# Weight sums of a seven-product feed-forward made by accumulating transfers, and a fourth pair of chunks by seven products

## The chip, the cores and the metric

The kernel runs on one core of a Trainium2 chip. The metric is the device time of one execution in microseconds, and the time of a kernel is the median of several executions. One execution was also taken by the hardware profiler; all rows below come from that one.

## The reference, cut to what matters

The program is a two-layer decoder trunk for 256 tokens of width 1024. Each layer has a feed-forward step, a token mixer, and a second feed-forward step, so there are four feed-forward stages with weights of their own. They are what the change touches.

```python
def swiglu(h, w_gate, w_up, w_down):
    return (jax.nn.silu(h @ w_gate) * (h @ w_up)) @ w_down

def rmsnorm(x, g):
    y = xf * lax.rsqrt(jnp.mean(xf * xf, axis=-1, keepdims=True) + RMS_EPS)
    return (y * g.astype(jnp.float32)).astype(x.dtype)

    f = swiglu(rmsnorm(x, g[0]), ffn_w_gate[layer, 0], ffn_w_up[layer, 0], ffn_w_down[layer, 0])
    x = x + 0.5 * rmsnorm(f, g[1])
    ... # token mixer
    f = swiglu(rmsnorm(x, g[4]), ffn_w_gate[layer, 1], ffn_w_up[layer, 1], ffn_w_down[layer, 1])
    x = x + 0.5 * rmsnorm(f, g[5])
```

The inner width is 2816, everything is float32.

## The kernel before, in words

**Units.** The inner width is cut into 11 chunks of 256. A chunk's gate and up columns together are 512 wide. The 256 tokens are two tiles of 128, called t = 0 and 1. The contraction over 1024 is eight slices of 128.

**Precision.** A float32 operand is split into `hi` (rounded by ScalarE, line 96) and `lo` (the rest, by VectorE, line 97). A product is three matmuls for each slice: hi·hi, hi·lo, lo·hi (`mm3`, lines 145 to 147, and `product`, lines 334 to 336). So each weight block of 512 x 512 that is loaded, 1 MiB, costs two ScalarE and two VectorE instructions of 128 x 1024 before TensorE can use it.

**Buffers.** A loaded block lies in one of five `raw` buffers of 1 MiB (`NRAW`), filled by two transfers of 512 KB (gate, up) on SyncE's queue (line 87). The `hi` and `lo` halves have nine slots each (`NW`); a block takes two of each. Products gather in two PSUM banks with the tag `mm`.

**Chunks done plainly.** `GU(t, c)` makes chunk c for token tile t: 8 slices x 3 = 24 matmuls of 128 x 512. `both` does it for both tiles, 48 matmuls, from two loaded blocks. Then `gated` makes silu(gate)·up, `T` transposes it on TensorE, and `Dn(t, c)` multiplies it by the chunk's rows of `w_down` (12 matmuls; the rows are one more block of 1 MiB for each chunk) into PSUM banks that gather over the whole stage.

**Pairs of chunks done by seven products.** For two neighbouring chunks a and b the token tiles are the rows, the halves of the contraction the middle, and the chunks the columns of a 2 x 2 block product. `M(i, a)` for i = 0 to 6 makes it by seven block products of 12 matmuls, 84 in place of 96. They need sums of weight blocks. With b11, b21 the two halves of chunk a and b12, b22 those of chunk b, VectorE makes four sums of 128 x 2048 for each pair, in place in the raw buffers:

```python
                nc.vector.tensor_tensor(w["b12"], w["b22"], w["b12"], op=ALU.subtract)   # L358, i == 1
                nc.vector.tensor_tensor(w["b11"], w["b12"], w["b11"], op=ALU.add)        # L359, i == 1
                nc.vector.tensor_tensor(w["b12"], w["b22"], w["b11"], op=ALU.subtract)   # L374, i == 4
                nc.vector.tensor_tensor(w["b21"], w["b21"], w["b11"], op=ALU.subtract)   # L382, i == 5
```

The sums of the token blocks (`S`) are made once for each stage. Results that are shared between outputs are combined on VectorE from PSUM (128 x 512: lines 364, 372, 379, 386, 392).

**Order.** `PAIRS = ((2, 3), (5, 6), (8, 9))`: chunks 0, 1, 4, 7, 10 are plain, so that a plain chunk stands between two pairs. A planner in `ffn` (`emit`, `settle`) writes out the order of `M`, `GU`, `T` and `Dn` from prices of each step (M 1, GU 2, both 4, Dn 1), so that a `Dn` comes between products. The framework's scheduler then gives each engine its queue, close to that order, and puts in the semaphore waits. GpSimd (POOL) has in the feed-forward stages only the power of each norm (line 182), and issues no transfer; all weights go over SyncE's queue.

Of the kernel before, what the change touches and what calls it, by code (L numbers as in the profile page):

```python
# [17 lines left out]
P = 128  # L18
# [16 lines left out]

PAIRS = ((2, 3), (5, 6), (8, 9))
SIDE, EARLY = 13, 5
# [11 lines left out]
def trunk(ctx, tc, x, norm_g, w_gate, w_up, w_down, ab_in, ab_out, conv_w, conv_b, conv_g, conv_bb,  # L49
# [10 lines left out]
    def ps_mm(name):  # L60
        return pp.tile([P, 512], F32, tag="mm", name=name, bufs=2)
# [58 lines left out]

    def load_block(l, j, c, half):

        def loads(raw):
            v = raw.rearrange("p (k g f) -> p k g f", k=4, g=2)
            return [(v[:, :, g, :], w[l, j, half * 512:half * 512 + 512, c * FC:(c + 1) * FC].rearrange("(k p) f -> p k f", p=P))
                    for g, w in ((0, w_gate), (1, w_up))]
        return load(loads, f"b{l}{j}_{c}_{half}")

# [121 lines left out]
    def ffn(l, j, pre, tail, hooks=()):  # L250
# [60 lines left out]


        S = {}

        def sums():
            (a11, a12), (a21, a22) = pre[0][3], pre[1][3]
            for n, dst, x, y, op in ((1, a22, a21, a22, ALU.add), (3, a21, a11, a21, ALU.subtract),
                                     (2, a11, a22, a11, ALU.subtract), (4, a12, a12, a11, ALU.subtract)):
                nc.vector.tensor_tensor(dst, x, y, op=op)
                d = sp.tile([P, 8, P], F32R, tag=f"S{n}" if n < 4 else "tg", name=f"S{n}_{l}{j}", bufs=1)  # L320
                split(dst, d[:, 0:4].rearrange("p a b -> p (a b)"), d[:, 4:8].rearrange("p a b -> p (a b)"))
                S[n] = (d[:, 0:4], d[:, 4:8])

# [14 lines left out]
        def M(i, a):  # L338
            b = a + 1
            n = f"{l}{j}_{a}"  # L340
            if i == 0:
                if not S:
                    sums()
                w = W[a] = {}
                w["m"] = sp.tile([P, 2, 512], F32, tag="cacc", name=f"m{n}")
                w["u"] = sp.tile([P, 2, 512], F32, tag="hpad", name=f"u{n}")
                w["b11"] = load_block(l, j, a, 0)
                units = split_raw(w["b11"], f"b11_{n}")
                w["b22"] = load_block(l, j, b, 1)
                w["b12"] = load_block(l, j, b, 0)  # L350
                w["X"] = ps_mm(f"gX{n}")
                product(w["X"], block(0, 0), units, True, False)
                nc.scalar.activation(w["m"][:, 0], w["X"], AF.Copy)
                return
            w = W[a]
            m1, m5, u1, u2 = w["m"][:, 0], w["m"][:, 1], w["u"][:, 0], w["u"][:, 1]
            if i == 1:
                nc.vector.tensor_tensor(w["b12"], w["b22"], w["b12"], op=ALU.subtract)  # L358
                nc.vector.tensor_tensor(w["b11"], w["b12"], w["b11"], op=ALU.add)  # L359
                units = split_raw(w["b11"], f"t2_{n}")  # L360
                w["b21"] = load_block(l, j, a, 1)
                w["Y"] = ps_mm(f"gY{n}")
                product(w["Y"], S[2], units, True, False)
                nc.vector.tensor_tensor(u1, w["Y"], m1, op=ALU.add)
            elif i == 2:
                units = split_raw(w["b21"], f"b21_{n}")
                product(w["X"], block(0, 1), units, False, True)
                gated(0, a, w["X"])
            elif i == 3:
                units = split_raw(w["b12"], f"t3_{n}")  # L370
                product(w["Y"], S[3], units, False, False)
                nc.vector.tensor_tensor(u2, w["Y"], m1, op=ALU.add)
            elif i == 4:
                nc.vector.tensor_tensor(w["b12"], w["b22"], w["b11"], op=ALU.subtract)  # L374
                units = split_raw(w["b12"], f"t1_{n}")
                w["X2"] = ps_mm(f"gX2{n}")
                product(w["X2"], S[1], units, True, False)
                nc.scalar.activation(m5, w["X2"], AF.Copy)
                nc.vector.tensor_tensor(u2, u2, m5, op=ALU.add)
                gated(1, b, u2)  # L380
            elif i == 5:
                nc.vector.tensor_tensor(w["b21"], w["b21"], w["b11"], op=ALU.subtract)  # L382
                units = split_raw(w["b21"], f"t4_{n}")
                product(w["Y"], block(1, 1), units, False, True)
                c = sp.tile([P, 512], F32, tag="va", name=f"c21_{n}", bufs=2)
                nc.vector.tensor_tensor(c, w["Y"], m1, op=ALU.add)
                gated(1, a, c)
            else:
                units = split_raw(w["b22"], f"b22_{n}")
                product(w["X2"], S[4], units, False, True)  # L390
                c = sp.tile([P, 512], F32, tag="va", name=f"c12_{n}", bufs=2)
                nc.vector.tensor_tensor(c, w["X2"], u1, op=ALU.add)
                gated(0, b, c)

# [9 lines left out]
        G.append((GU, 0, e))  # L404
        makes = {2: (0, 0), 4: (1, 1), 5: (1, 0), 6: (0, 1)}
        price = {M: 1.0, GU: 2.0, both: 4.0, T: 0.1, Dn: 1.0}
# [510 lines left out]
```

## Time and profile before

| | |
|---|---|
| median of 3 runs | 992.99 us |
| lowest and highest run | 986.86 and 993.05 us |
| the profiled execution's own time | 989.26 us |
| its span, first to last instruction | 987.3 us |
| mean granted TensorE clock | 0.994 |
| busy: TensorE, VectorE, ScalarE, GpSimd | 953.1, 837.7, 579.4, 97.7 us |
| moved over SyncE's queue | 174.5 MB |

The profiled execution's time lies 2.0 us above its span, and 3.7 us below the median. Busy times of TensorE count matmuls that overlap as pipelined, so an issue distance is read from starts that follow one another, not from durations.

### The profile page before, as it was taken

What the parts mean: (1) busy time and instruction counts of PE and PEld (TensorE: products, weight loads), DVE (VectorE), ACT (ScalarE), POOL (GpSimd) and SP (SyncE); (2) the same over time, 40 slices, a digit from 0 to 9 for tenths busy, and PEclk for the clock granted to TensorE, in tenths of its full rate; (3) what the DMA queues carried; (4) which work ended last, traced back from release to release, by engine and by line L of the source; (5) the groups of instructions that cost most, each with busy time, mean ns of one, the idle gap of its engine ahead of it and who ended that gap; (6) DMA issues with size and microseconds to landing.
All of it is one profiled execution on the core that took longest, in us unless ns stands there. A gap on an engine that the chain in (4) does not pass through costs nothing.

```text
span 987.3 us, 11853 instructions
## 1 busy us (share of the span) xinstructions
PE 953.1 (97%) x4350; PEld 759.0 (77%) x4352; DVE 837.7 (85%) x1022; ACT 579.4 (59%) x845; POOL 97.7 (10%) x104
## 2 busy tenths in 40 slices
PE   7999999999888999999999999999999989999997
PEld 5777888787657688878778887877787778887875
DVE  6999999679887999988789999996757489999883
ACT  7575656563535656656576756575555466656561
POOL 0100000039961000000000000000000010000000
PEclk9999999999989999999999999999999999999999
DMA  9657647456007339383862658385564142838341
GB/s 313 209 184 230 218 167 282 161 177 232 1 18 239 91 107 315 122 262 121 284 213 86 200 183 275 109 311 162 209 220 144 43 127 86 275 120 288 107 168 43
DMA packets 121754, 175.32 MB, mean 178 GB/s; under 512 B 4481, under 2 KB 96321, under 8 KB 121696
## 3 DMA queue, kind: packets, MB, share of 16 engines
q1 hardware_dynamic: 121536, 174.50, 53.7%
q8 instruction: 34, 0.56, 0.2%
q14 instruction: 24, 0.20, 0.1%
q10 hardware_dynamic: 160, 0.07, 0.0%
HBM read 173.50 MB, written 1.05 MB: 177 GB/s over the span
## 4 chain that ended last, share of the span: by engine, by line
PE 84%; DVE 8%; ACT 3%; DMA 2%; issue 2%; POOL 1%; SPq 0%; POOLq 0%; DVEq 0%; ACTq 0%
PE f L145 8%; PE f L146 8%; PE f L147 8%; PE gu L147 6%; PE gu L145 6%; PE gu L146 6%; PE gX L334 4%; PE gX L336 4%; PE gX L335 4%; PE gY L334 3%; PE gY L335 3%; PE gY L336 3%; PE hT L153 2%; PE cd L145 2%; PE cd L146 2%
## 5 line engine op out<-in xcount | busy, mean ns | idle before, releaser
L145 PE MATMUL f<-hi_dn,hs 128*128 128x512 f32 x352 | 139.7, 400 | 0.5 <-ACT hs L157 0.5
L146 PE MATMUL f<-lo_dn,hs 128*128 128x512 f32 x352 | 138.0, 392 | 0.0
L147 PE MATMUL f<-hi_dn,hs 128*128 128x512 f32 x352 | 137.5, 393 | 0.0
L96 ACT ACTIVATE hi_t<-raw_b 128x1024 fp32r<-128x1024 f32 x96 | 98.1, 1053 | 60.2 <-DVE raw_b L374 47.1
L97 DVE TENSOR_TENSOR lo_t<-raw_b,hi_t 128x1024 fp32r<-128x1024 f32 x96 | 114.5, 1220 | 14.5 <-ACT hi_t L96 14.5
L97 DVE TENSOR_TENSOR lo_dn<-raw_dn,hi_dn 128x1024 fp32r<-128x1024 f32 x88 | 105.7, 1219 | 9.0 <-ACT hi_dn L96 8.9
L96 ACT ACTIVATE hi_dn<-raw_dn 128x1024 fp32r<-128x1024 f32 x88 | 91.7, 1055 | 36.4 <-PE gu L147 26.2
L97 DVE TENSOR_TENSOR lo_gu<-raw_gu,hi_gu 128x1024 fp32r<-128x1024 f32 x80 | 96.6, 1218 | 8.3 <-ACT hi_gu L96 8.0
L96 ACT ACTIVATE hi_gu<-raw_gu 128x1024 fp32r<-128x1024 f32 x80 | 83.5, 1055 | 27.9 <-PE m L147 11.7
L97 DVE TENSOR_TENSOR lo_b<-raw_b,hi_b 128x1024 fp32r<-128x1024 f32 x72 | 86.3, 1219 | 2.5 <-ACT hi_b L96 2.3
L96 ACT ACTIVATE hi_b<-raw_b 128x1024 fp32r<-128x1024 f32 x72 | 74.8, 1057 | 21.4 <-PE gu L147 12.9
L145 PEld LDWEIGHTS f<-hi_dn,hs 128*128 128x128 f32 x352 | 65.7, 188 | 17.2 <-ACT hs L157 4.4
L147 PEld LDWEIGHTS f<-hi_dn,hs 128*128 128x128 f32 x352 | 66.1, 188 | 15.3 <-DVE hs L158 1.7
L146 PEld LDWEIGHTS f<-lo_dn,hs 128*128 128x128 f32 x352 | 66.2, 188 | 13.8 <-DVE lo_dn L97 1.0
L157 ACT ACTIVATE hs<-hT 128x256 fp32r<-128x256 f32 x88 | 32.2, 377 | 54.9 <-PE hT L153 54.9
L145 PE MATMUL gu<-hi_gu,xh_l1f 128*128 128x512 f32 x160 | 63.6, 397 | 0.0
L146 PE MATMUL gu<-lo_gu,xh_l1f 128*128 128x512 f32 x160 | 63.4, 396 | 0.0
L147 PE MATMUL gu<-hi_gu,xl_l1f 128*128 128x512 f32 x160 | 62.2, 393 | 0.0
L158 DVE TENSOR_TENSOR hs<-hT,hs 128x256 fp32r<-128x256 f32 x88 | 36.0, 418 | 20.4 <-ACT hs L157 20.0
L282 ACT ACTIVATE sg<-gu 128x256 f32<-128x256 f32 x38 | 14.5, 381 | 42.1 <-PE gu L147 39.3
L334 PE MATMUL gY<-hi_t,S 128*128 128x512 f32 x96 | 38.6, 402 | 0.0
L336 PE MATMUL gY<-hi_t,S 128*128 128x512 f32 x96 | 38.0, 396 | 0.0
(361 smaller groups left out, 2240.7 us busy)
## 6 DMA issues: line engine op xcount, KB each, us to landing
raw_dn<-in_ffn_w_down_dram SPq DMA_DIRECT2D x44, 1024.0 KB, 5.0
raw_b<-in_ffn_w_gate_dram SPq DMA_DIRECT2D x48, 512.0 KB, 4.7
raw_b<-in_ffn_w_up_dram SPq DMA_DIRECT2D x48, 512.0 KB, 6.2
raw_gu<-in_ffn_w_gate_dram SPq DMA_DIRECT2D x38, 512.0 KB, 4.2
raw_gu<-in_ffn_w_up_dram SPq DMA_DIRECT2D x38, 512.0 KB, 5.2
raw_ab<-in_ab_w_in_dram SPq DMA_DIRECT2D x10, 1024.0 KB, 6.9
raw_cd<-in_cd_w_in_dram SPq DMA_DIRECT2D x10, 1024.0 KB, 5.1
raw_abo<-in_ab_w_out_dram SPq DMA_DIRECT2D x4, 1024.0 KB, 5.5
```

The lines of the kernel that those rows point to most:

```text
L96: nc.scalar.activation(hi, r, AF.Copy)
L97: nc.vector.tensor_tensor(lo, r, f32v(hi), op=ALU.subtract)
L145: nc.tensor.matmul(ps, xh, wh, start=first, stop=False)
L146: nc.tensor.matmul(ps, xh, wl, start=False, stop=False)
L147: nc.tensor.matmul(ps, xl, wh, start=False, stop=last)
L153: nc.tensor.transpose(ps[:, i * P:(i + 1) * P], src[:, i * P:(i + 1) * P], ident)
L157: nc.scalar.activation(hi, ps, AF.Copy)
L158: nc.vector.tensor_tensor(lo, ps, f32v(hi), op=ALU.subtract)
L282: nc.scalar.activation(sg, ps[:, 0:FC], AF.Silu, scale=1.0 if r is None else r)
L334: nc.tensor.matmul(ps, A[0][:, k, :], wh[:, o], start=first and k == 0, stop=False, **tc_skip)
L335: nc.tensor.matmul(ps, A[0][:, k, :], wl[:, o], start=False, stop=False, **tc_skip)
L336: nc.tensor.matmul(ps, A[1][:, k, :], wh[:, o], start=False, stop=k == 3, **tc_skip)
```

## The change

Four things change at once.

1. `PAIRS` becomes `((2, 3), (4, 5), (6, 7), (8, 9))`: chunks 4 and 7, plain before, become part of pairs, and no plain chunk stands between pairs any more. This holds in all four feed-forward stages.
2. The sums change their signs (so that each weight sum is an addition), and three of the four sums of a pair are made by transfers with `accum_op=add`, issued from GpSimd's queue: `t = b12 + b11` (b12 loaded by SyncE, b11 added from HBM by two transfers of 512 KB), `b22 += b12` (again two from HBM), and `b21 += t` (one transfer of 1 MiB within SBUF). One sum, `t += b22`, stays on VectorE. So b11 and b12 are each read from HBM a second time: 2 MiB more for each pair.
3. The seven products come in another order: b11, t1, b21, b22, t2, t3, t4. The three that gather in one bank (`Y`) now follow one another, i = 4, 5, 6; before they were i = 1, 3, 5.
4. In SyncE's queue the load of b12 into `t` stands ahead of that of b11, and the three others follow at once in step 0.

```diff
-PAIRS = ((2, 3), (5, 6), (8, 9))
+PAIRS = ((2, 3), (4, 5), (6, 7), (8, 9))
...
+    def add_block(raw, l, j, c, half):
+
+        for dst, src in block_of(l, j, c, half)(raw):
+            tc.keep_in_program_order(nc.gpsimd.dma_start(dst, src, accum_op=ALU.add))
...
-            for n, dst, x, y, op in ((1, a22, a21, a22, ALU.add), (3, a21, a11, a21, ALU.subtract),
-                                     (2, a11, a22, a11, ALU.subtract), (4, a12, a12, a11, ALU.subtract)):
+            for n, dst, x, y, op in ((1, a22, a21, a22, ALU.subtract), (3, a21, a11, a21, ALU.subtract),
+                                     (2, a11, a22, a11, ALU.subtract), (4, a12, a12, a11, ALU.add)):
...
+                w["t"] = load_block(l, j, b, 0)
+                add_block(w["t"], l, j, a, 0)
                 w["b11"] = load_block(l, j, a, 0)
                 units = split_raw(w["b11"], f"b11_{n}")
+                w["b21"] = load_block(l, j, a, 1)
                 w["b22"] = load_block(l, j, b, 1)
-                w["b12"] = load_block(l, j, b, 0)
...
             if i == 1:
-                nc.vector.tensor_tensor(w["b12"], w["b22"], w["b12"], op=ALU.subtract)
-                nc.vector.tensor_tensor(w["b11"], w["b12"], w["b11"], op=ALU.add)
-                units = split_raw(w["b11"], f"t2_{n}")
-                w["b21"] = load_block(l, j, a, 1)
-                w["Y"] = ps_mm(f"gY{n}")
-                product(w["Y"], S[2], units, True, False)
-                nc.vector.tensor_tensor(u1, w["Y"], m1, op=ALU.add)
+                units = split_raw(w["t"], f"t1_{n}")
+                w["X2"] = ps_mm(f"gX2{n}")
+                product(w["X2"], S[1], units, True, False)
+                nc.scalar.activation(m5, w["X2"], AF.Copy)
...
             elif i == 3:
-                units = split_raw(w["b12"], f"t3_{n}")
+                units = split_raw(w["b22"], f"b22_{n}")
+                nc.vector.tensor_tensor(w["t"], w["t"], w["b22"], op=ALU.add)
+                add_block(w["b22"], l, j, b, 0)
+                tc.keep_in_program_order(nc.gpsimd.dma_start(w["b21"], w["t"], accum_op=ALU.add))
+                product(w["X2"], S[4], units, False, True)
+            elif i == 4:
+                units = split_raw(w["t"], f"t2_{n}")
+                w["Y"] = ps_mm(f"gY{n}")
+                product(w["Y"], S[2], units, True, False)
+                nc.vector.tensor_tensor(u1, w["Y"], m1, op=ALU.add)
+                gated(0, b, made(w["X2"], u1, ALU.subtract, "c12"))
+            elif i == 5:
+                units = split_raw(w["b22"], f"t3_{n}")
                 product(w["Y"], S[3], units, False, False)
                 nc.vector.tensor_tensor(u2, w["Y"], m1, op=ALU.add)
-            elif i == 4:
-                nc.vector.tensor_tensor(w["b12"], w["b22"], w["b11"], op=ALU.subtract)
-                units = split_raw(w["b12"], f"t1_{n}")
...
-                nc.vector.tensor_tensor(u2, u2, m5, op=ALU.add)
+                nc.vector.tensor_tensor(u2, m5, u2, op=ALU.subtract)
                 gated(1, b, u2)
-            elif i == 5:
-                nc.vector.tensor_tensor(w["b21"], w["b21"], w["b11"], op=ALU.subtract)
+            else:
                 units = split_raw(w["b21"], f"t4_{n}")
                 product(w["Y"], block(1, 1), units, False, True)
...
-        makes = {2: (0, 0), 4: (1, 1), 5: (1, 0), 6: (0, 1)}
+        makes = {2: (0, 0), 4: (0, 1), 5: (1, 1), 6: (1, 0)}
```

## Rows read from the trace of the kernel before

**Rows 1.** The page's head: span, and busy time of each engine.

```profile
span 987.3 us, 11853 instructions
...
PE 953.1 (97%) x4350; PEld 759.0 (77%) x4352; DVE 837.7 (85%) x1022; ACT 579.4 (59%) x845; POOL 97.7 (10%) x104
```

**Rows 2.** Windows of the four feed-forward stages: engines' busy time, clock, DMA share, GB/s.

```profile
24.70:214.00 189.30, 186.33 (x845) 149.38 (x845) 170.65 (x199) 113.84 (x163) 5.79 (x7) 1.00 0.61 206
320.00:505.00 185.00, 182.11 (x820) 145.64 (x819) 164.43 (x185) 115.53 (x168) 2.74 (x5) 1.00 0.57 184
505.00:690.00 185.00, 183.85 (x827) 147.81 (x825) 165.92 (x188) 114.94 (x164) 3.04 (x4) 1.00 0.60 194
790.00:987.30 197.30, 187.82 (x837) 151.15 (x835) 164.54 (x190) 112.89 (x163) 4.72 (x5) 0.99 0.46 152
```

**Rows 3.** Timeline of TensorE, first stage: one product's first matmul and the next step's.

```profile
151.90 0.40 PE L334 MATMUL gX<-hi_b,xh_l0n 128*128 128x512 f32 x1
...
154.65 0.39 PE L145 MATMUL f<-hi_dn,hs 128*128 128x512 f32 x1
```

**Rows 4.** Windows, third stage and second: pair with plain chunk; dense loads; no loads.

```profile
587.12:635.51 48.39, 48.29 (x217) 39.22 (x216) 44.26 (x46) 29.46 (x39) 0.00 (x0) 1.00 0.62 203
330.00:345.00 15.00, 15.00 (x71) 11.78 (x70) 14.09 (x20) 8.10 (x15) 0.55 (x1) 1.00 0.06 11
...
599.00:614.00 15.00, 15.00 (x68) 12.08 (x67) 14.55 (x18) 11.44 (x14) 0.00 (x0) 1.00 1.04 334
```

**Rows 5.** Groups of instructions, whole span: busy, mean ns, idle before.

```profile
L97 DVE TENSOR_TENSOR lo_t<-raw_b,hi_t 128x1024 fp32r<-128x1024 f32 x96 | 114.5, 1220 | 14.5 <-ACT hi_t L96 14.5
L96 ACT ACTIVATE hi_t<-raw_b 128x1024 fp32r<-128x1024 f32 x96 | 98.1, 1053 | 60.2 <-DVE raw_b L374 47.1 <-PE f L147 6.1 <-DVE raw_b L359 5.9
...
L158 DVE TENSOR_TENSOR hs<-hT,hs 128x256 fp32r<-128x256 f32 x88 | 36.0, 418 | 20.4 <-ACT hs L157 20.0
...
L359 DVE TENSOR_TENSOR raw_b<-raw_b,raw_b 128x2048 f32<-128x2048 f32 x12 | 27.5, 2289 | 0.2
...
L285 DVE TENSOR_TENSOR h<-c,sg 128x256 f32<-128x256 f32 x24 | 10.0, 418 | 0.0
...
L364 DVE TENSOR_TENSOR u<-gY,m 128x512 f32<-128x512 f32 x12 | 8.3, 688 | 0.0
```

**Rows 6.** The page's DMA issues: count, KB each, median us to landing.

```profile
raw_b<-in_ffn_w_gate_dram SPq DMA_DIRECT2D x48, 512.0 KB, 4.7
raw_b<-in_ffn_w_up_dram SPq DMA_DIRECT2D x48, 512.0 KB, 6.2
```

**Rows 7.** Timeline of SyncE's queue, third stage: first and last load of a pair.

```profile
604.45 0.37 SPq L87 DMA_DIRECT2D raw_b<-in_ffn_w_gate_dram  x1
604.86 0.51 SPq L87 DMA_DIRECT2D raw_b<-in_ffn_w_up_dram  x1
...
621.62 0.50 SPq L87 DMA_DIRECT2D raw_b<-in_ffn_w_up_dram  x1
```

**Rows 8.** Timeline of GpSimd, second stage: all that it does there.

```profile
330.95 0.55 POOL L182 TENSOR_TENSOR v_pl0f<-v_pl0f,mhalf 128x1 f32<-128x1 f32 x1 [3.23 <-DVE v_pl0f L181]
496.66 0.55 POOL L182 TENSOR_TENSOR v_ql1f<-v_ql1f,mhalf 128x1 f32<-128x1 f32 x1 [165.16 <-DVE v_ql1f L181]
```

**Rows 9.** Timeline of TensorE, third stage: last matmuls into bank Y.

```profile
595.13 0.40 PE L336 MATMUL gY<-hi_t,S 128*128 128x512 f32 x1
...
612.25 0.39 PE L336 MATMUL gY<-hi_t,xl_l1f 128*128 128x512 f32 x1
```

**Rows 10.** Timeline of VectorE, same stretches: the reads of bank Y.

```profile
595.63 0.69 DVE L364 TENSOR_TENSOR u<-gY,m 128x512 f32<-128x512 f32 x1
...
613.60 0.68 DVE L386 TENSOR_TENSOR c<-gY,m 128x512 f32<-128x512 f32 x1
```

**Rows 11.** The chain that ended last: pieces on the weight sums (start, us).

```profile
59.55 2.20 DVE raw_b L374
62.35 2.21 DVE raw_b L382
...
90.36 2.20 DVE raw_b L359
...
434.42 2.29 DVE raw_b L358
```

More of the change, by code (lines that the diff above doesn't have):

```diff
@@ L119, in prep_gu, with block_of @@
         return [(hi[:, o:o + 512], lo[:, o:o + 512]) for hi, lo in units for o in (0, 512)]
-    def load_block(l, j, c, half):
+    def block_of(l, j, c, half):
         def loads(raw):
@@ L126, in loads, with load_block @@
                     for g, w in ((0, w_gate), (1, w_up))]
-        return load(loads, f"b{l}{j}_{c}_{half}")
+        return loads
+    def load_block(l, j, c, half):
+        return load(block_of(l, j, c, half), f"b{l}{j}_{c}_{half}")
+    def add_block(raw, l, j, c, half):
+        for dst, src in block_of(l, j, c, half)(raw):
+            tc.keep_in_program_order(nc.gpsimd.dma_start(dst, src, accum_op=ALU.add))
     def prep_in(w, c, name):
@@ L340, in M, with made @@
             n = f"{l}{j}_{a}"
+            def made(x, y, op, name):
+                c = sp.tile([P, 512], F32, tag="va", name=f"{name}_{n}", bufs=2)
+                nc.vector.tensor_tensor(c, x, y, op=op)
+                return c
             if i == 0:
@@ L369, in M @@
             elif i == 3:
-                units = split_raw(w["b12"], f"t3_{n}")
+                units = split_raw(w["b22"], f"b22_{n}")
[11 more added lines that the diff above has]
+                units = split_raw(w["b22"], f"t3_{n}")
                 product(w["Y"], S[3], units, False, False)
                 nc.vector.tensor_tensor(u2, w["Y"], m1, op=ALU.add)
-            elif i == 4:
-                nc.vector.tensor_tensor(w["b12"], w["b22"], w["b11"], op=ALU.subtract)
-                units = split_raw(w["b12"], f"t1_{n}")
-                w["X2"] = ps_mm(f"gX2{n}")
-                product(w["X2"], S[1], units, True, False)
-                nc.scalar.activation(m5, w["X2"], AF.Copy)
-                nc.vector.tensor_tensor(u2, u2, m5, op=ALU.add)
+                nc.vector.tensor_tensor(u2, m5, u2, op=ALU.subtract)
                 gated(1, b, u2)
-            elif i == 5:
-                nc.vector.tensor_tensor(w["b21"], w["b21"], w["b11"], op=ALU.subtract)
+            else:
                 units = split_raw(w["b21"], f"t4_{n}")
                 product(w["Y"], block(1, 1), units, False, True)
[L385 to L393, printed above, removed]
+                gated(1, a, made(w["Y"], m1, ALU.add, "c21"))
         inside = {c for pair in pairs for c in pair}
```

## The prediction, made before the changed kernel ran

> **What bounds the kernel now.** I read the page's head first, then the windows of the stages, then timelines of one pair. TensorE is busy 953 of 987 us [rows 1]; in the two middle feed-forward stages it is busy 182 and 184 of 185 us at a granted clock of 1.00 [rows 2], so nothing else ends late there. The matmuls are issued back to back: a product's twelve take 154.65 - 151.90 = 2.75 us, 0.229 us each [rows 3]. The reader is to see how little room is left beside that. VectorE is busy 164 to 171 us of each stage [rows 2], and over one pair and the plain chunk after it 44.3 of 48.4 us, with the DMA engines at 0.62 [rows 4]. So TensorE sets the time, VectorE is 9% behind it, DMA has some 40% left, and GpSimd is empty from 331.5 to 496.7 us [rows 8].
>
> **The parts of the change.**
>
> Matmuls. Per stage, one more pair does 84 in place of 96: 12 x 0.229 = 2.75 us, over four stages 11.0 us. This is on the path, since TensorE is never late: the sure gain.
>
> VectorE. Per stage nine sums of 2.29 us go (three of four, three pairs), -20.6 us. The fourth pair brings one sum (2.29), six more split instructions (seven blocks at two each for four blocks: 14 for 8, 6 x 1.22 = 7.3) and five combinations (5 x 0.69 = 3.4): +13.0 [rows 5]. Net -7.6 us a stage. None of that is on the path where TensorE is full; ScalarE's waits for the sum of line 374 (47.1 us) [rows 5] go too, and it has room (115 of 185) [rows 2]. On the chain four pieces of weight sums stand, 2.20 + 2.21 + 2.20 + 2.29 = 8.9 us [rows 11]; three of four such sums leave, so up to 7 us more could go. I take 0 in the sum, because TensorE was full around them, and 7 as the far end.
>
> Within a pair, though, VectorE becomes tight. TensorE's time for one pair with its four Dn: 84 + 48 = 132 x 0.229 = 30.2 us, and four T. A T costs (48.39 - 204 x 0.229)/6 = 0.27 us (84 + 48 + 72 matmuls and six T stand in that window) [rows 4], so 31.3 us. VectorE's: 18 splits (22.0), one sum (2.3), five combinations (3.4), four gatings and four hT splits of 0.42 (3.4) = 31.1 us [rows 5]. The plain chunk that stood between pairs let it catch up, and is gone; with no waits it just keeps pace.
>
> Transfers, the price that decides. Loads run densely at 334 GB/s with all engines taken (share 1.04), 1.049 MB / 334 GB/s = 3.14 us for each MiB block [rows 4]. A pair still loads six blocks on SyncE's queue (four of gate and up, two of w_down): 18.8 us of its 31.3. New are three accumulating MiB. No row shows one, nor any transfer issued by GpSimd. Bounds from the nearest row, the load of the same block: it must at least bring its source, 3.14 us (no gain is possible here, bytes are added and none taken away: the load of each block stays); it also reads the destination and writes it back, and if each of the three passes cost as much as a load, 9.42 us. I take two loads' worth, 6.28 us: the write is what a load does anyway, and the destination's read is one more pass of the same bytes through the same engines. So a pair asks for 18.8 + 18.8 = 37.7 us of DMA, with bounds 28.3 and 47.1, against TensorE's 31.3. It decides at (31.3 - 18.8)/3 = 4.2 us, 1.33 loads.
>
> The Trainium skill (Collectives: The Full Stack, The bandwidth ceiling) says that a reducing transfer puts two read descriptors for each chunk on one ring, and so runs at half of a copy's rate; the sum by that would be the same 37.7 us. No run here shows it yet. Its page DMA: Bandwidth & Descriptors (Issuing engines are not separate DMA queues) says that transfers of all issuers run on the same 16 engines; without that rule the two 18.8 us would lie side by side and neither would bind.
>
> Latency tells the same. The accumulations stand in one order on GpSimd's queue, pinned there: b22 += b12 (waits for VectorE's sum of step 3), b21 += t, then the next pair's t += b11 (waits for its load). Behind the first wait stands the next pair's accumulation, for which its product 1 waits. The loop from one pair's sum to the next's: three accumulations 18.8 us; a landing of 4.7 - 1.57 = 3.1 us beyond the moving of 512 KB [rows 6]; then the splits of t, b21, b22 (6 x 1.22 + 1.05), a w_down split (2.44), some 2 us of small work, the sum 2.29: 15.1 us. Together 37.0 us, if SyncE's loads take nothing from it.
>
> GpSimd's issues, five for each pair: between SyncE's 0.37 us [rows 7] and a whole landing, 4.7 [rows 6], each: 2 to 24 us of an engine that is empty [rows 8]. Cover enough at either end; I take the low one. In SyncE's queue the load into t is moved ahead of b11's, 3.1 us of delay for product 0. Before, a pair's first load is issued 604.45 and product 0 runs at 635.5, 31 us later [rows 4, 7], which hides it. The cover shrinks, as t holds its buffer from its load to the end of b21 += t.
>
> Bank Y. Products 4, 5, 6 gather in one bank, and VectorE reads it between them, so product 5 can't write before that read ends; before, another product lay between. By the planner's rule with the new list, 4 and 5 of the pair (4, 5), and 5 and 6 of the last three pairs, stand with no Dn between. A bare read costs from the last matmul's slot to the read's end: 596.32 - 595.36 = 1.0 us, or 614.28 - 612.48 = 1.8 where VectorE had something in hand [rows 9, 10]. Four a stage, 16 x 1.4 = 22 us; where the scheduler moves a Dn or the next product 0 between, half of them, 10. If TensorE waits for weights anyway, these lie inside that wait: 0 in the likeliest case.
>
> **Sum.** 989.3 - 11.0 + 12 x (37.7 - 31.3) = 989.3 - 11 + 77 = 1055. Twelve, because there are three steps between pairs in each stage; the first pair's blocks and its first accumulation come early, while the engines idle (share 0.06) [rows 4]. The profiled execution lies 3.7 us under the median, so 1059.
>
> **Rivals.**
>
> An accumulation costs about a load (up to 1.2). Then DMA needs 28 to 31 us of 31.3, the loop 27.6, and all is hidden: 978.3 us, plus bank Y's 10 to 22: 988 to 1000, in runs 992 to 1004: for the most part no change. For: the mean share is only 0.6 [rows 2]. Against: the destination's bytes move too.
>
> The other side: as above, and the scheduler covers bank Y; then 978 + 3.7 = 982, and with the 7 us off the chain 975. It needs a price under 4.2 us and VectorE without waits at 31.1 of 31.3; before it idled 4.1 us of 48.4 [rows 4], which speaks against.
>
> Between, 1.5 loads: DMA 32.9 us, 12 x 1.6 = 19, with bank Y between nothing and 22 us: 1001 to 1023 in runs.
>
> Three passes at a load's price, or accumulations that don't overlap one another: 47.1 us a pair, all pairs late: 978.3 + 16 x 15.8 = 1231, 1235 in runs. At 2.5 loads, 42.4 us: 978.3 + 16 x 11.1 + 3.7 = 1160.
>
> **Chances.** 1% is about what a measurement can tell here, 983 to 1003 as no change. Two loads' worth, 1025 to 1150: 0.42, its own range. 1.5 loads, 1001 to 1025: 0.12. Hidden but for bank Y: 0.21. Hidden and faster: 0.12. Dearer, over 1150: 0.13. So faster 0.12, same 0.21, slower 0.67. Range 978 to 1150: it leaves out the dearer case and some 0.05 below.
>
> **What would show it.** Right: TensorE's idle in the pairs ends on the weights' splits, those on DMA; the DMA share near 1 from chunk 2 to 9; a MiB accumulation of 6 us or more and a pair in some 38 us; TensorE's matmul count less by 48. The bank's part: gaps of 1 to 2 us between products 4, 5 and 6. Wrong: a share under 0.85 with TensorE still full (accumulations cheap), or waits on GpSimd's issue itself with DMA idle, which I price at nothing.

## The result: 18% slower, and the profile after

The changed kernel takes 1165.62 us (median of 4, 1160.13 to 1166.9; a fifth run took 1168.73) against 990.88 for the kernel before in the same runs: a ratio of 1.1767, interval [1.1712, 1.1821]. The direction was forecast, the time was not: it lies 15.6 us above the upper end of the range and 107 us above the value. The profiled execution spans 1158.1 us against 987.3 [rows 1], 170.8 more; that is the sum that has to be explained.

The page of the changed kernel: span and busy times (these answer to [rows 1]), the DMA queues with packets, megabytes and share of 16 engines, the shares of the chain that ended last, the costliest waits' groups, and the DMA issues with the median us to landing, which answer to [rows 6].

```profile
span 1158.1 us, 12126 instructions
...
PE 989.1 (85%) x4304; PEld 777.2 (67%) x4304; DVE 812.7 (70%) x1034; ACT 610.0 (53%) x877; POOL 195.5 (17%) x184
...
q1 hardware_dynamic: 121536, 174.50, 44.6%
q0 software_dynamic: 36096, 50.34, 25.6%
...
PE 43%; DMA 30%; DVE 15%; ACT 5%; issue 5%; POOL 2%; SPq 0%; POOLq 0%; ACTq 0%; DVEq 0%
...
L96 ACT ACTIVATE hi_t<-raw_b 128x1024 fp32r<-128x1024 f32 x128 | 131.4, 1053 | 206.5 <-DMA raw_b<-in_ffn_w_up_dram 154.1
...
L343 PE MATMUL gY<-hi_t,S 128*128 128x512 f32 x128 | 62.8, 490 | 73.5 <-DVE u L393 73.5
...
raw_b<-in_ffn_w_gate_dram SPq DMA_DIRECT2D x64, 512.0 KB, 8.2
raw_b<-in_ffn_w_up_dram SPq DMA_DIRECT2D x64, 512.0 KB, 9.9
raw_b<-in_ffn_w_gate_dram POOLq DMA_DIRECT2D x32, 512.0 KB, 6.2
raw_b<-in_ffn_w_up_dram POOLq DMA_DIRECT2D x32, 512.0 KB, 9.1
raw_b<-raw_b POOLq DMA_DIRECT2D x16, 1024.0 KB, 12.5
```

Read it in this order. The chain is now 43% TensorE and 30% DMA. Queue q0 holds the 48 accumulated MiB: 25.6% of 1158.1 us is 296.5 us of all 16 engines, **6.18 us a MiB** where 6.28 was taken. The idle time is in front of ScalarE's splits of the summed blocks (206.5 us, 154.1 of them until the up half of an accumulation has landed); and bank Y's first matmul waits 73.5 us, by the name, for VectorE's read of the bank, which is a false trail (below). SyncE's plain loads land in 8.2 and 9.9 us.

Now the pairs. Windows of the second stage: engines' busy time and matmuls, clock, DMA share, GB/s. The first three run from one pair's accumulation of b22 to the next pair's, one period each; the rest are stretches inside.

```profile
404.80:452.28 47.48, 38.29 (x155) 29.95 (x154) 30.45 (x33) 24.10 (x32) 6.07 (x6) 0.93 0.78 199
452.28:496.01 43.73, 32.79 (x135) 25.72 (x134) 28.52 (x33) 20.86 (x28) 6.07 (x5) 0.84 0.86 217
496.01:541.15 45.14, 34.70 (x138) 27.02 (x137) 29.18 (x33) 21.17 (x28) 6.10 (x5) 0.89 0.82 209
420.50:432.00 11.50, 8.21 (x32) 6.01 (x31) 7.36 (x10) 3.26 (x5) 2.59 (x2) 0.89 1.14 287
441.40:444.70 3.30, 3.30 (x12) 2.65 (x11) 1.92 (x2) 2.35 (x3) 0.00 (x0) 0.72 0.01 4
```

The three periods ask for 0.78 x 47.48 = 37.0, 37.6 and 37.0 us of DMA, against 37.7 forecast: the work is right. But the periods are 43.7 to 47.5 us: the DMA engines are idle for 14 to 22% of each, full in one stretch (1.14) and empty in another (0.01). Over all four stages the twelve periods add up to 540.4 us, a mean of 45.0; TensorE is busy 34.9 us of one. The last line of the same view, asked for all twelve:

```profile
sum 540.41, PE 419.28 PEld 329.71 DVE 351.88 ACT 265.61 POOL 73.22; mean PE 34.94 PEld 27.48 DVE 29.32 ACT 22.13 POOL 6.10
```

The chain of the second stage, in order of time (start, us, what):

```profile
409.29 1.24 DVE lo_dn L97
410.54 9.43 DMA raw_b<-in_ffn_w_gate_dram
...
420.53 1.22 POOL raw_b L135
421.75 13.16 DMA raw_b<-in_ffn_w_up_dram
435.01 1.07 ACT hi_t L96
...
449.29 2.30 DVE raw_b L385
...
453.78 16.04 DMA raw_b<-raw_b
...
470.71 8.06 DMA raw_b<-in_ffn_w_up_dram
```

It goes from the split of a w_down block, which frees a buffer, to the load of t, its accumulation and its split, then through the pair to the sum of line 385, to b21's accumulation, and over the buffer that this frees to the next pair's loads. It is not quite the loop that the prediction put at 37.0 us: there t's accumulation followed b21's at once, and no load stood between them. Its two accumulations take 13.2 and 16.0 us here.

SyncE's queue shows why they lie as they do:

```profile
389.91 3.48 SPq L87 DMA_DIRECT2D raw_dn<-in_ffn_w_down_dram  x2
410.54 0.37 SPq L87 DMA_DIRECT2D raw_b<-in_ffn_w_gate_dram  x1
...
418.70 0.37 SPq L87 DMA_DIRECT2D raw_b<-in_ffn_w_gate_dram  x1
...
424.95 6.34 SPq L87 DMA_DIRECT2D raw_dn<-in_ffn_w_down_dram  x2
```

The load into t, at the front of a pair's loads, finds no free raw buffer until 410.54 (the two before it went to w_down at 389.91). When it is in, at 420, the other loads have buffers too: five MiB are issued from 418.70 on, in the same stretch as t's accumulation. That is the window with a share of 1.14.

An accumulation without company stands in the DMA view of 373 to 390 us (the first pair's t):

```profile
raw_b<-in_ffn_w_gate_dram POOLq DMA_DIRECT2D x1, 512.0 KB, 6.0
raw_b<-in_ffn_w_up_dram POOLq DMA_DIRECT2D x1, 512.0 KB, 7.8
```

6.0 and 7.8 us. With company there are two cases. t's accumulation runs beside the loads: in eight of the twelve periods its up half lands 11.9 to 14.8 us after its issue (421.75 above: 13.16). b21's stands behind b22's in the same queue, and in twelve of the sixteen pairs it lands in 12.4 to 13.5 us with few loads beside it: that is the work of two accumulated MiB, 2 x 6.18 = 12.4. Window of one such case, from b21's issue to its landing (columns as above):

```profile
542.65:555.08 12.43, 12.43 (x57) 10.17 (x56) 5.77 (x7) 4.37 (x6) 2.02 (x2) 1.00 1.04 196
```

In the other four pairs a MiB of loads runs beside it, as at 453.78 above, and it takes 15.5 to 16.2 us.

### The profile page after: what moved, and what is told of

It is laid out like the page before. It is cut to its first block, busy times and chain, and to the rows that moved or that the text cites. A ratio compares the mean times of both kernels' runs of the same rounds, so it can differ in the third digit from the quotient of the medians.

```text
span 1158.1 us, 12126 instructions
## 1 busy us (share of the span) xinstructions
PE 989.1 (85%) x4304; PEld 777.2 (67%) x4304; DVE 812.7 (70%) x1034; ACT 610.0 (53%) x877; POOL 195.5 (17%) x184
## 3 DMA queue, kind: packets, MB, share of 16 engines
q0 software_dynamic: 36096, 50.34, 25.6%
## 4 chain that ended last, share of the span: by engine, by line
PE 43%; DMA 30%; DVE 15%; ACT 5%; issue 5%; POOL 2%; SPq 0%; POOLq 0%; ACTq 0%; DVEq 0%
DMA raw_b<-in_ffn_w_up_dram 12%; DMA raw_b<-raw_b 11%; DMA raw_b<-in_ffn_w_gate_dram 4%; PE f L153 3%; PE f L154 3%; PE gu L155 3%; PE gu L154 3%; PE f L155 3%; PE gu L153 3%; DVE lo_t L97 3%; DVE lo_b L97 2%; PE gY L343 2%; PE gY L345 2%; PE gY L344 2%; DVE lo_dn L97 2%
## 5 line engine op out<-in xcount | busy, mean ns | idle before, releaser
L97 DVE TENSOR_TENSOR lo_t<-raw_b,hi_t 128x1024 fp32r<-128x1024 f32 x128 | 153.0, 1220 | 171.0 <-ACT hi_t L96 170.6
L96 ACT ACTIVATE hi_t<-raw_b 128x1024 fp32r<-128x1024 f32 x128 | 131.4, 1053 | 206.5 <-DMA raw_b<-in_ffn_w_up_dram 154.1
L135 POOL DMA_DIRECT2D raw_b<-in_ffn_w_gate_dram x32 | 41.5, 1298 | 529.8 <-DVE lo_b L97 308.5
L97 DVE TENSOR_TENSOR lo_b<-raw_b,hi_b 128x1024 fp32r<-128x1024 f32 x96 | 115.3, 1219 | 21.2 <-ACT hi_b L96 20.5
L343 PE MATMUL gY<-hi_t,S 128*128 128x512 f32 x128 | 62.8, 490 | 73.5 <-DVE u L393 73.5
L161 PE MATMUL hT<-cst,h 128*128 128x128 f32 x176 | 37.6, 299 | 58.0 <-DVE h L293 58.0
L343 PEld LDWEIGHTS gY<-hi_t,S 128*128 128x128 f32 x128 | 29.7, 232 | 84.9 <-issue 43.6
L97 DVE TENSOR_TENSOR lo_gu<-raw_gu,hi_gu 128x1024 fp32r<-128x1024 f32 x48 | 57.6, 1219 | 12.4 <-ACT hi_gu L96 12.1
L96 ACT ACTIVATE hi_gu<-raw_gu 128x1024 fp32r<-128x1024 f32 x48 | 49.9, 1051 | 29.8 <-PE gY L345 14.0
L345 PE MATMUL gY<-hi_t,S 128*128 128x512 f32 x128 | 59.9, 468 | 0.0
L344 PE MATMUL gY<-lo_t,S 128*128 128x512 f32 x128 | 59.8, 467 | 0.0
L135 POOL DMA_DIRECT2D raw_b<-in_ffn_w_up_dram x32 | 52.8, 1649 | 35.6 <-DMA raw_b<-in_ffn_w_up_dram 35.3
```

Of the source, the lines that this page charges most:

```text
L96: nc.scalar.activation(hi, r, AF.Copy)
L97: nc.vector.tensor_tensor(lo, r, f32v(hi), op=ALU.subtract)
L135: tc.keep_in_program_order(nc.gpsimd.dma_start(dst, src, accum_op=ALU.add))
L161: nc.tensor.transpose(ps[:, i * P:(i + 1) * P], src[:, i * P:(i + 1) * P], ident)
L343: nc.tensor.matmul(ps, A[0][:, k, :], wh[:, o], start=first and k == 0, stop=False, **tc_skip)
L344: nc.tensor.matmul(ps, A[0][:, k, :], wl[:, o], start=False, stop=False, **tc_skip)
```

## The experiments

The theory after the trace: the price is right, and the time is lost because accumulations are waited for in two places, between pairs (t) and inside a pair (b22, b21). Rivals: the new order of products; bank Y; the fourth pair by itself; GpSimd's issues. Each kernel was timed in three rounds; "plain" means an accumulating transfer turned into an ordinary one of the same bytes, from the same queue, with every engine's order unchanged (a plain chunk remains one that is done without the seven products). The kernel before took 990.0 to 992.4 us in the rounds of the experiments, so differences of a few us between them carry little.

**All transfers plain.**

```diff
-            tc.keep_in_program_order(nc.gpsimd.dma_start(dst, src, accum_op=ALU.add))
+            tc.keep_in_program_order(nc.gpsimd.dma_start(dst, src))
...
-                tc.keep_in_program_order(nc.gpsimd.dma_start(w["b21"], w["t"], accum_op=ALU.add))
+                tc.keep_in_program_order(nc.gpsimd.dma_start(w["b21"], w["t"]))
```

> The changed kernel with its five accumulating transfers of a pair turned into plain ones from the same queue, to the same places, with the same waits (the sums are left out, so the weights are wrong). Theory 1, the chain of accumulations: an accumulated MiB costs the DMA engines 6.2 us where a plain one costs 3.1, and the three of a pair lie one behind the other on the path from one pair's sum to the next; with plain ones a pair falls from 45.0 us to some 35, the kernel to 1010 to 1060. Rival, the waits and buffers alone (GpSimd's issue, five raw buffers, the load into t that waits for a free one): a pair stays over 41 us and the kernel over 1110. Rival, the new order of the products (bank Y): also over 1110.

1017.07 us, 1.027 [1.0247, 1.0293]. The accumulating alone costs 148.5 us; the rest of the change, with the fourth pair, the new order and five plain transfers with their waits, costs 26. Its page (queue, issues), then the window of one period of the third stage, and the last line of that view for all twelve periods:

```profile
q0 software_dynamic: 11520, 50.34, 14.8%
...
raw_b<-in_ffn_w_gate_dram POOLq DMA_DIRECT2D x32, 512.0 KB, 4.5
raw_b<-in_ffn_w_up_dram POOLq DMA_DIRECT2D x32, 512.0 KB, 6.2
raw_b<-raw_b POOLq DMA_DIRECT2D x16, 1024.0 KB, 7.8
```

```profile
561.49:597.90 36.41, 34.64 (x154) 27.61 (x153) 29.89 (x33) 23.89 (x32) 3.52 (x5) 1.00 0.76 260
...
sum 420.05, PE 389.21 PEld 307.26 DVE 348.74 ACT 266.22 POOL 42.31; mean PE 32.43 PEld 25.61 DVE 29.06 ACT 22.18 POOL 3.53
```

14.8% of 1018.5 us over 48 MiB is 3.14 us a MiB, so accumulating costs 1.97 times as much. The Trainium skill (Collectives: The Full Stack, The bandwidth ceiling) has a reducing transfer at half of a copy's rate; this case's 1.97 agrees. All twelve periods of this kernel add up to 420.0 us, a mean of 35.0, although TensorE has 31.3 by the prediction's sum: it is busy 32.4 us of a period and idle for the rest. In the changed kernel it is busy 34.9 us of 45.0. So of the 10.0 us between the two, 7.5 are idle time of TensorE and 2.5 are the same matmuls going slower, at a granted clock of 0.84 to 0.93 in its periods against 0.95 to 1.00 here.

**The sums back on VectorE, in the new order** (three for the transfers that go, beside line 385's):

```diff
-                add_block(w["t"], l, j, a, 0)
...
+                nc.vector.tensor_tensor(w["t"], w["t"], w["b11"], op=ALU.add)
...
-                add_block(w["b22"], l, j, b, 0)
-                tc.keep_in_program_order(nc.gpsimd.dma_start(w["b21"], w["t"], accum_op=ALU.add))
...
+                nc.vector.tensor_tensor(w["b22"], w["t"], w["b11"], op=ALU.subtract)
...
+                nc.vector.tensor_tensor(w["b21"], w["b21"], w["t"], op=ALU.add)
```

> The changed kernel, its four pairs and its new order of products, with all four sums on VectorE and no transfer from GpSimd. Theory 1: the loss of the change is the accumulations', so it goes; what is left is VectorE, 31.1 + 3 x 2.29 = 38.0 us for a pair against TensorE's 31.3, up to 16 x 6.7 = 107 us over 982, less what the start of each stage gives: 1010 to 1080. Rival, the new order (bank Y read between products 4, 5 and 6): the loss stays, over 1110.

1053.2 us, 1.0629 [1.0613, 1.0644].

**The kernel before with four pairs, nothing else.**

```diff
-PAIRS = ((2, 3), (5, 6), (8, 9))
+PAIRS = ((2, 3), (4, 5), (6, 7), (8, 9))
```

> The kernel before with the four pairs alone: old order of the products, all sums on VectorE. It costs the fourth pair by itself: 11 us less of TensorE, and VectorE at 38.0 us for a pair against 31.3. Theory 1 with VectorE as the bound: 1010 to 1085. If the nine slots of hi and lo and the plain chunks at both ends cover VectorE's lag: 980 to 1000.

1048.87 us, 1.0579 [1.0547, 1.0612]: within 4 us of the kernel above. So with the sums on VectorE the new order costs 4 us at most, and the fourth pair costs 58 us by itself. VectorE is then busy 911.0 of 1045.5 us. By the prediction's own rows a pair with four sums is 31.1 + 3 x 2.29 = 38.0 us of VectorE against 31.3 of TensorE, and -11 + 12 x 6.7 = 69. The accumulations were to take these 38.0 down to 31.1; they make the kernel 112 us slower than the sums do (1165.62 - 1053.2).

**No read of bank Y between its products** (the gathered values are left out of two combinations):

```diff
-                nc.vector.tensor_tensor(u1, w["Y"], m1, op=ALU.add)
+                nc.vector.tensor_tensor(u1, m5, m1, op=ALU.add)
...
-                nc.vector.tensor_tensor(u2, w["Y"], m1, op=ALU.add)
+                nc.vector.tensor_tensor(u2, u1, m1, op=ALU.add)
```

> The changed kernel in which VectorE doesn't read bank Y between products 4, 5 and 6: u1 and u2 are made from m1 and m5 alone (the products' shares of u1 and u2 are left out). Theory: TensorE's waits for line 393 in the profile of the changed kernel (73 us) are VectorE's queue waiting for an accumulation, so they move elsewhere: 1145 to 1165. Rival, that the new order itself costs what those waits show: 1080 to 1110.

1159.95 us, 1.1707 [1.1646, 1.1768]: about 6 us less, and the intervals overlap. The 73.5 us under "gY <- DVE u L393" were not the bank. VectorE's reads in the changed kernel, one pair (timeline, idle before and releaser in brackets):

```profile
465.75 2.36 DVE L97 TENSOR_TENSOR lo_t<-raw_b,hi_t 128x1024 fp32r<-128x1024 f32 x2 [8.67 <-ACT hi_t L96]
470.93 2.36 DVE L97 TENSOR_TENSOR lo_t<-raw_b,hi_t 128x1024 fp32r<-128x1024 f32 x2 [2.82 <-ACT hi_t L96]
...
474.34 0.68 DVE L393 TENSOR_TENSOR u<-gY,m 128x512 f32<-128x512 f32 x1
```

The read of line 393 stands in VectorE's queue behind two splits that wait 8.67 and 2.82 us. They wait for ScalarE's half of the split, and that for an accumulation: b21's lands at 453.78 + 16.04 = 469.82, and the second split starts 1.1 us later. The read's name is on TensorE's wait, the transfer is the cause.

**One accumulation plain at a time**: t's (line 363), b22's (line 386), b21's (line 387).

```diff
-                add_block(w["t"], l, j, a, 0)
+                add_block(w["t"], l, j, a, 0, plain=True)
```

> The changed kernel with only t's two accumulating transfers made plain (t is then b11 alone; same queues, same order of every engine). The plain form of all three gave back 148 us. If the accumulations form one loop from pair to pair, or if the DMA engines' total is what counts, each third of the 9.3 us taken off a pair gives a third: 1105 to 1125. Rival, that the waits inside a pair decide (the split of a sum stands in ScalarE's and VectorE's queues ahead of other work while b22's and b21's accumulations land, as the three-pair kernel suggests): t, which has the most time to land, gives little, 1145 to 1165.

1107.72 us, 1.1174 [1.1126, 1.1221]: 58 back.

```diff
-                add_block(w["b22"], l, j, b, 0)
+                add_block(w["b22"], l, j, b, 0, plain=True)
```

> The changed kernel with only b22's two accumulating transfers made plain (b22 is then b12 alone). Loop or total: a third, 1105 to 1125. Waits inside a pair: b22's is issued at the sum of step 3, needed at step 5, and b21's stands behind it in the same queue, so it gives the most: 1060 to 1100.

1145.04 us, 1.154 [1.1486, 1.1594]: 20.6 back.

```diff
-                tc.keep_in_program_order(nc.gpsimd.dma_start(w["b21"], w["t"], accum_op=ALU.add))
+                tc.keep_in_program_order(nc.gpsimd.dma_start(w["b21"], w["t"]))
```

> The changed kernel with only the transfer b21 += t made plain (b21 is then t). Loop or total: a third, 1105 to 1125. Waits inside a pair: it lands last of the pair's two and holds two raw buffers, on which the next pair's loads wait, so it gives about what b22's does: 1070 to 1120.

1128.38 us, 1.1376 [1.1318, 1.1435]: 37 back. Only t's result fits what one loop or one total would give; b22's lies above and b21's just above all that was expected. So all three matter, t's the most. Together they give 116 of the 148.5; 33 more come only when all three are plain. So their costs overlap: with one gone, the others still bind. How they do was not taken apart.

**The old three pairs with the new transfers.**

```diff
-PAIRS = ((2, 3), (4, 5), (6, 7), (8, 9))
+PAIRS = ((2, 3), (5, 6), (8, 9))
```

> The changed kernel with the old three pairs: accumulations and new order as changed, a plain chunk between two pairs. Theory 1: the loop from pair to pair takes about 45 us, and TensorE has 47.7 us of work between two sums, so the loop is nearly hidden: 990 to 1030. If the DMA engines' total binds: nine blocks loaded and three accumulated are 9 x 3.1 + 3 x 6.2 = 46.5 us of 47.7, the same time. Rival, the order of the products: twelve pairs keep three quarters of the loss, 1100 to 1125.

1087.41 us, 1.0969 [1.0951, 1.0988], a miss of 57 us, and 13 us under the rival's range too: a plain chunk between pairs was thought to hide the loop. It hides most of the part between pairs, as the runs after this one show; the following rows are what it can't hide. ScalarE's timeline in one pair of the third stage, then TensorE's:

```profile
611.47 2.00 ACT L96 ACTIVATE hi_t<-raw_b 128x1024 fp32r<-128x1024 f32 x2 [8.45 <-DMA raw_b<-in_ffn_w_up_dram]
613.38 0.36 ACT L165 ACTIVATE hs<-hT 128x256 fp32r<-128x256 f32 x1
616.78 2.00 ACT L96 ACTIVATE hi_t<-raw_b 128x1024 fp32r<-128x1024 f32 x2 [3.04 <-DMA raw_b<-raw_b]
```

```profile
613.79 0.79 PE L153 MATMUL f<-hi_dn,hs 128*128 128x512 f32 x1 [5.51 <-ACT hs L165]
```

b22's accumulation is issued in step 3 and its split stands first in ScalarE's queue, which idles 8.45 us for it. Behind it stands hs, which a w_down product needs and whose input has long been there; TensorE waits 5.51 us for hs, then the next split waits 3.04 us for b21. This lies between products of one pair, whatever stands between pairs.

**Three pairs, all plain; b22 and b21 plain; t plain.**

```diff
-            tc.keep_in_program_order(nc.gpsimd.dma_start(dst, src, accum_op=ALU.add))
+            tc.keep_in_program_order(nc.gpsimd.dma_start(dst, src))
...
-PAIRS = ((2, 3), (4, 5), (6, 7), (8, 9))
+PAIRS = ((2, 3), (5, 6), (8, 9))
```

(This is the all-plain one; the other two keep the accumulation of t, or of b22 and b21.)

> Three pairs with the accumulating transfers made plain (the sums are left out). If the price is the cause there as with four pairs: 990 to 1010. If the new order of the products, or where the loads stand in the queue, is part of it: over 1030.

> Three pairs, t's accumulation kept, b22's and b21's transfers plain (their sums are left out); the order of every engine as in the three-pair kernel. If the waits inside the pair, for what is issued at step 3 and needed at steps 5 and 6, cost the three-pair kernel its time: 1010 to 1030. If t's does: 1065 to 1087.

> Three pairs, t's transfers plain (its sum is left out), b22's and b21's accumulating. The other side of the same question: waits inside the pair 1065 to 1087, t's accumulation 1010 to 1030.

1008.3 (1.0171 [1.0139, 1.0203]), 1020.68 (1.0309 [1.0262, 1.0355]) and 1073.92 (1.0842 [1.0797, 1.0887]). With three pairs b22 and b21 are worth 66.7 us and t 13.5, together 80.2 of 79.1: additive. With four, t is worth 58. That tells the two places apart.

**t's load and accumulation earlier**, in step 2 of the pair before:

```diff
+            if i == 2 and (a + 2, a + 3) in pairs:
+                early_t[a + 2] = make_t(a + 2)
...
-                w["t"] = load_block(l, j, b, 0)
-                add_block(w["t"], l, j, a, 0)
+                w["t"] = early_t.pop(a) if a in early_t else make_t(a)
```

> The changed kernel with the load into t and its accumulation moved to step 2 of the pair ahead, for the last three pairs of each stage. Theory 1b: the next pair's accumulation no longer stands behind this pair's two and beside the burst of loads, so the loop is cut: 1080 to 1130. Rival, the total of the engines' work: 1150 to 1175; and slower than that if the one buffer less holds up the loads of w_down.

1107.53 us, 1.1185 [1.1128, 1.1243]: 58 back, as much as a plain t. Windows of two of its periods:

```profile
607.38:647.40 40.02, 36.43 (x156) 28.90 (x155) 29.65 (x33) 24.09 (x32) 6.11 (x5) 0.96 0.94 236
647.40:689.77 42.37, 32.48 (x134) 25.97 (x133) 28.51 (x33) 21.11 (x28) 6.12 (x5) 0.84 0.89 223
```

With the same bytes these periods fall to 40.0 and 42.4 us at shares of 0.94 and 0.89, nearer the 37.7 that the prediction took for all of them; the third of a stage has no early t left to bring, and the mean of all twelve is 40.4. So t's part between pairs is for the most part a matter of when, not of how much.

**One more raw buffer in place of one slot for split weights; the same with t early; t early with three pairs; t early with all transfers plain.**

```diff
-NW = 9
-NRAW = 5
+NW = 8
+NRAW = 6
```

> The changed kernel with six raw buffers in place of five, paid for by eight slots of hi and lo in place of nine. Theory 1b: the loads of the next pair wait for a raw buffer (t holds one until b21 += t has landed), come in a burst then, and its accumulation into t shares the DMA engines with that burst, so a pair takes 45 us where the engines need 37.7; with a sixth buffer a pair nears 38 to 41: 1090 to 1125. Rival, the DMA engines' total or the chain itself: within 10 us of 1166. The lost slot can cost some us in either case.

> Four pairs with the accumulation into t two steps into the pair ahead, and six raw buffers with eight slots of hi and lo. Early t alone gave 58 us, the sixth buffer alone 23. If both are one cause (the loads of the next pair come late), the two together give little more than the better one: 1095 to 1115. If they are two, 81 us: 1075 to 1095.

> Three pairs with accumulations, and t's load and accumulation moved to step 2 of the pair ahead, so with a plain chunk and more between. If the late t is what cost the three-pair kernel its 97 us: 1000 to 1040. If the waits for b22's and b21's accumulations inside a pair did: 1065 to 1090.

> Four pairs, plain transfers in place of the accumulating ones (the sums are left out), t's load and transfer in step 2 of the pair ahead. With the DMA work at 28 us for a pair and t no longer late, TensorE's 31.3 us should bind: 975 to 995. If VectorE's 31.1 us with its waits, or bank Y, is what is left of e1's 26 us: 1005 to 1020.

1142.96 (1.1516 [1.1461, 1.157]), 1120.5 (1.1295 [1.1248, 1.1342]), 1082.98 (1.0921 [1.0888, 1.0955]) and 1027.32 (1.0329 [1.0268, 1.039]). A buffer gives 23 us back where t waits for one, less than expected, and costs 13 where t comes early, slower than either theory had it. That the slot that went for it is missed there would explain it, but was not shown. With three pairs an early t is worth some 4 us, no more than the spread between rounds: there the rest is inside the pairs. With plain transfers an early t gains nothing: the medians lie 10 us apart the wrong way, the intervals overlap, and the gain that had been expected stays away unexplained.

**Sums on GpSimd** (kernel before, four pairs; one sum, then two of four):

```diff
-                nc.vector.tensor_tensor(w["b21"], w["b21"], w["b11"], op=ALU.subtract)
+                nc.gpsimd.tensor_tensor(w["b21"], w["b21"], w["b11"], op=ALU.subtract)
```

> The kernel before with four pairs in the old order, and one of the four sums (line 382, b21 - b11) computed by GpSimd in place of VectorE, with no accumulating transfer. Theory: VectorE's 38.0 us for a pair bound the four-pair kernel at 1049; with 35.7 it comes to 1010 to 1030. Rival, that VectorE and GpSimd hinder one another (GpSimd's own 128x512 sums took 1.36 us in the mixer, so a sum takes some 5.4 us): 1040 to 1060.

```diff
-                nc.vector.tensor_tensor(w["b12"], w["b22"], w["b12"], op=ALU.subtract)
+                nc.gpsimd.tensor_tensor(w["b12"], w["b22"], w["b12"], op=ALU.subtract)
```

> As the one before, with the sum of line 358 (b22 - b12) on GpSimd too: VectorE at 33.4 us for a pair against TensorE's 31.3, GpSimd at some 11. Theory: 980 to 1005. Rival, that GpSimd's slower sum stands on the path to the sum of line 359 and product 1, or that the two engines hinder one another: 1030 to 1070.

1079.82 (1.088 [1.0838, 1.0923]) and 1148.23 (1.157 [1.1522, 1.1619]): 31 and 99 us slower than with all four on VectorE, both misses. Groups of the first, then VectorE's and GpSimd's timelines beside one such sum:

```profile
L97 DVE TENSOR_TENSOR lo_t<-raw_b,hi_t 128x1024 fp32r<-128x1024 f32 x128 | 216.4, 1724 | 20.0 <-ACT hi_t L96 20.0
...
L97 DVE TENSOR_TENSOR lo_b<-raw_b,hi_b 128x1024 fp32r<-128x1024 f32 x96 | 115.6, 1219 | 1.2 <-ACT hi_b L96 1.1
...
L382 POOL TENSOR_TENSOR raw_b<-raw_b,raw_b 128x2048 f32<-128x2048 f32 x16 | 78.6, 4912 | 505.7 <-DVE lo_b L97 505.7
```

```profile
594.45 6.79 DVE L97 TENSOR_TENSOR lo_t<-raw_b,hi_t 128x1024 fp32r<-128x1024 f32 x2
```

```profile
594.67 5.49 POOL L382 TENSOR_TENSOR raw_b<-raw_b,raw_b 128x2048 f32<-128x2048 f32 x1 [27.57 <-DVE lo_b L97]
```

The splits of the group in which some run beside GpSimd's sum (lo_t) take 1724 ns on the mean in place of 1220 [rows 5], 128 x 0.504 = 64.5 us of VectorE, 1.8 times the 16 x 2.29 = 36.6 that the moved sum frees; VectorE is busy 941.6 us, against 911.0 with all four sums on it. Those of lo_b keep their 1219. Whether the later sum also holds up its product was not taken apart.

## Why the prediction was wrong in size

**Right.** TensorE's 48 weight loads and matmuls go (4304 against 4352 loads). An accumulated MiB costs 6.18 us of the engines, where 6.28 was taken between 3.14 and 9.42, and a pair 37.0 to 37.6 where 37.7 was. The rivals of a cheap accumulation, hidden or at 1.5 loads, fall with that, and so does that of three passes. Bank Y is worth next to nothing beside the other waits (6 us, within the noise), as taken. GpSimd's issues take 1.28 to 2.04 us each in place of the 0.37 taken, within their bounds; they are not wholly free, with 3.2% of the chain from 404 to 545 us, 4.5 us. The rival at 2.5 loads named 1160 us, near what was measured, but by luck: its price of 7.85 us a MiB is not the one found.

**The step that failed** is the term 12 x (37.7 - 31.3) = 77: it makes the pair as long as its DMA work, as if the engines would be full from chunk 2 to 9. The prediction's own test for that, a share near 1 and a pair of 38 us, failed: 0.82 and 45.0. The term is 12 x (45.0 - 31.3) = 164. The plain kernel splits it. Of the 13.7 us, 3.7 stand there as well (35.0), with no accumulation, 44 us in all: TensorE has some 1.1 us more in a period than the 31.3 worked out, and idles the rest; that VectorE "just keeps pace" was said for no waits alone. The other 10.0 us, 120 in all, come from accumulating. With the 11 us of fewer matmuls this makes -11 + 44 + 120 = 153 of the 170.8. The last 18 lie outside the twelve periods; in the plain kernel the same sum (-11 + 44 = 33 for 31.2) leaves none. They lie behind the last pairs. From a stage's first gate-and-up matmul to its first accumulation into b22 the second and third stages take 37.9 and 41.1 us in both kernels, so there the first pairs were free, as taken. But from the last one (1098.39) to the end of the span the changed kernel takes 59.7 us and the plain one 53.2: TensorE idles there once, 4.9 us before bank Y's first matmul, behind splits that wait for the last pair's own b22 and b21, and the twelve steps between pairs don't count that.

Three things were left out of the step, all shown by runs. First, a transfer's landing: the loop took one of 3.1 us beyond the moving, "if SyncE's loads take nothing from it". They do: t's accumulation mostly lands in 11.9 to 14.8 us beside them, and in 6.0 and 7.8 without. Second, when t can be loaded: in its time for moving the load, the prediction had 31 us of cover, and named that t holds its buffer, but not that it must first get one. The early t (58 us) and the three pairs (t worth 13.5) show that place. Third, the cover inside a pair: b22's and b21's results are wanted two and three products after their sum, the two take 12.4 us even with few loads beside them, and in-order queues turn a late split into a wait of everything behind it; with three pairs that is 66.7 of 79.1 us. The prediction had these two only as a part of its loop from sum to sum, not as a wait inside the pair.

**What stays open.** TensorE is busy 989.1 us with 48 matmuls fewer, where 953.1 less the 11.0 would be 942.1: 47 us more. 34 of them are more than the plain kernel's 955.1 too, and 12 x 2.5 = 30 of these lie in the twelve periods. The rows after a pause show why that can be. TensorE's timeline at the wait for the accumulation of 421.75, with the window 441.40 to 444.70 above:

```profile
435.81 0.39 PE L345 MATMUL gY<-hi_t,xl_l0f 128*128 128x512 f32 x1
439.04 0.41 PE L161 MATMUL hT<-cst,h 128*128 128x128 f32 x2 [2.85 <-DVE h L293]
...
440.55 0.63 PE L344 MATMUL gY<-lo_t,xh_l0f 128*128 128x512 f32 x1
440.98 0.63 PE L345 MATMUL gY<-hi_t,xl_l0f 128*128 128x512 f32 x1
...
443.63 0.39 PE L345 MATMUL gX<-hi_b,xl_l0f 128*128 128x512 f32 x1
443.86 0.40 PE L343 MATMUL gX<-hi_b,xh_l0f 128*128 128x512 f32 x1
```

Soon after 2.85 us of idle time the matmuls follow at 0.43 us, and from 443.63 on at 0.23: the lower of its two levels, 1.2 GHz, then the upper again. How much of the 47 us lies on the path was not measured apart. Open is also what idles TensorE in the pairs of the plain kernel (some 2.6 us each). By the profile's waits it stands 20.6 us before transposes and 10.7 us before bank Y's first matmul, both for VectorE; whether VectorE's work, its waits for transfers or the bank is behind that, no run took apart. The same goes for the 1.7% that three pairs with plain transfers still lose, and for the 33 us that the three accumulations cost together beyond their single effects.

None of the versions beats the kernel before; the best, three pairs with plain transfers, leaves the sums out and still takes 1.017 of its time. A stage's fourth pair saves TensorE 2.75 us, less than it cost with any way of making the weight sums that was run. What the first three pairs gain was not run.

## What to carry to other kernels

A queue's work divided by its rate is only a lower bound for a step: take it as the period only if the transfers can be issued early enough to fill the engines, and ask for each result how many steps lie between its issue and its use, against its landing with all that runs beside it and stands ahead of it in its queue (here 12 to 16 us, where t's alone took 6 to 8). A plain step that seems to be spare time between two dense ones is cover: see what it hides before filling it. Where an in-order engine waits for a transfer, the wait shows up under the name of whatever is behind it, so look at what stands ahead in that queue.

## What the runs showed of the hardware

An accumulating transfer into on-chip memory costs the DMA engines 6.18 us a MiB, a plain one of the same shape 3.14. Beside them SyncE's loads landed in 8.2 and 9.9 us in place of 4.7 and 6.2 [rows 6]; with plain transfers they landed in 6.2 and 10.0, so the rise of the second is there without the accumulating too.

GpSimd's idle time was not free for sums: one of 128x2048 takes 4.91 us there against 2.29 on VectorE [rows 5], and two splits beside it took 6.79 us in place of 2.36. The Trainium skill (SBUF — State Buffer, Who interferes with whom) says that a VectorE instruction with two inputs in that memory contends with a GpSimd instruction that reads it, over a read port that they share; the rows above agree, with 1724 against 1219 ns.
